# A PEER expert product with its two token halves in one 512-column product, and gate stores in sixteen pieces

## The chip, the core and the metric

The kernel runs on one core of a Trainium2 chip. The metric is the device time of one launch in microseconds; the value for the kernel before is 1862.34 us, the median of three runs (1862.03 to 1863.49). Engine names: TensorE (PE in the rows, PEld for its weight loads), VectorE (DVE), ScalarE (ACT), GpSimd (POOL), SyncE (SP, which only issues DMAs). ScalarE and GpSimd issue DMAs too.

## The reference

One layer over 256 latent tokens (and 256 context tokens) of width 2048: adaLN modulation, a token mixer with RG-LRU scans and a spatial gating unit, an output projection, then a PEER expert layer and a final RMSNorm. The change lies in the expert layer:

```
q   = h @ w_q                                  # per token: 8 heads x 2 halves x 128
s1, s2 = q half 0 · k1, q half 1 · k2          # 128 scores each, per head
v1, i1 = top16(s1);  v2, i2 = top16(s2)
sc, flat = top16(v1[i] + v2[j])                # 16 of 256 pairs, per head
idx = e1 * 128 + e2;  g = softmax(sc)          # 128 (expert, gate) pairs per token, of 16384 experts
act = gelu(h · u_tab[idx])
out = sum over pairs of g * act * v_tab[idx]
```

## The kernel before, in words

**Number format.** Products have fp32 accuracy by splitting each operand into a high part and a low part (`split`, L245 to L261: ScalarE copies the high part, L252, VectorE subtracts to get the low part, L253). `mm3` (L280 to L283) makes three TensorE products from it: high weights with high tokens, high weights with low tokens, low weights with high tokens. Weights arrive as 1 MB tiles in four raw slots, loaded by SP (`emit_load`, L92), each when the split of the tile four places earlier is done. Split halves rotate through five slots of 1024 columns; a tile is split two steps before it is used.

**The expert stage.** The first expert product is dense: all 16384 experts for all 256 tokens, in 128 steps of 128 experts (`u_step`, L1164). A step is 16 blocks of `mm3`, 48 products of 256 columns, into one of four banks; then ScalarE takes the Gelu from the bank (L1176) and stores it (L1177) as 256 columns of the DRAM table `agd`, whose row holds for one expert the activations and the gates of the 256 tokens.

**The fill.** Each step ends with `fill`, which issues some 3000 ns worth of side work, by estimates written into the generators (`beneath`, L1147): the routing (top-16 and softmax, VectorE nearly alone), `list_tables`, the dense gate matrix (`gates`, L1035), the place of each used expert in a compact list (`places`), and the list itself (`make_list`). The work per step does not depend on how long a step takes. `gates` goes in blocks of 8 tokens: two one-hot matrices (L1021) and one scaled (L1030) on VectorE, 24 products of 128 columns (L1041, L1044), and two ScalarE copies into one of two chunk buffers `GC` (L1051). After 8 blocks (64 tokens, one chunk; four chunks in all) ScalarE issues four stores of 1 MB each, in runs of 256 bytes (L1056).

**The second expert product.** The list has 92 tiles of 128 experts. For each, GpSimd fetches the rows of the value table (`gather`, L910) and of `agd` (`act_rows`, L913) by indirect DMA; gate times activation (L1187) gives the weights, split by L1196 and L1201, and `mm3` with 512 columns adds into the output banks. Table fetches 0 to 3 are issued from the fill, the following ones by `emit_load` when the slot that they fill is free. Between the stages stands a branch on the list's overflow (`tc.If`, L1255), not taken with this input: two row fetches are issued ahead of it, the next ones behind it.

**Order.** The program is written out by hand; each engine, and each engine's DMA queue, works through its own instructions in program order and waits on semaphores.

Of the kernel before, what the change touches and what calls it, by code (L numbers as in the profile page):

```python
# [14 lines left out]
ALU = mybir.AluOpType  # L15
# [35 lines left out]
def layer_kernel(ctx: ExitStack, tc: tile.TileContext, I, out, dbg=None):  # L51
# [15 lines left out]
    def q_(off, n):  # L67
        assert O_Q + off + n <= N_F
        return fa[:, O_Q + off:O_Q + off + n]

    def r_(off, n):
        assert O_RP + off + n <= N_R
        return ra[:, O_RP + off:O_RP + off + n]
# [3 lines left out]
    def small(n):  # L77
        o = sm_used[0]
        sm_used[0] += n
        assert sm_used[0] <= N_SM  # L80
        return fa[:, o:o + n]
# [6 lines left out]
    order = []  # L88
    pos = [0]
    loaded = set()  # L90

    def emit_load(i):  # L92
        if i < len(order):
            loaded.add(i)
            key, parts = order[i]
            if parts is None:
                if key[1] + N_RAW < N_L:
                    gather(key[1] + N_RAW)
                return
            base = O_RAW + (i % N_RAW) * D  # L100
            for o, n, src in parts:
                nc.sync.dma_start(fa[:, base + o:base + o + n], src)
# [173 lines left out]
    def behind():  # L276
        if pending:
            pending.pop()()
# [507 lines left out]
    G.dma_start(KY[:, 1024:2048], I["k2t"])  # L786


    HH = r_(0, 4096).rearrange("p (k t) -> p k t", k=KD)
    HL = r_(4096, 4096).rearrange("p (k t) -> p k t", k=KD)  # L790
    HF = [q_(256 * i, 256) for i in range(4)]
    def norm2(k):
        b = pb[4 + k % 4]
# [88 lines left out]
    LIST, LIST2 = (small(N_L).bitcast(U32) for _ in range(2))  # L882
    AGR = [q_(12288 + 512 * i, 512) for i in range(4)]
    WP = [dg2, eg[:, 0:256]]
    pidx = small(1)
    flag = small(3)

# [22 lines left out]
    def gather(n):  # L910
        by_index(v_raw(n), v_rows, LISTV[:, SEQ[n]:SEQ[n] + 1], NE - 1)
# [120 lines left out]

    def gates():  # L1035
        def products(b):
            counts = pb[4 + b // NB][:, 0:P]
            oj, og = pair(b, P)
            for i in range(TB):
                oa = OHA[b % 2][:, i, :]  # L1040
                TE.matmul(counts, oa, oj[:, i, :], start=b % NB == 0 and i == 0,  # L1041
                          stop=b % NB == NB - 1 and i == TB - 1, skip_group_check=True)
                for q in range(2):
                    TE.matmul(pb[6 + i // 4][:, (i % 4) * P:(i % 4 + 1) * P], oa, og[:, i, q, :],  # L1044
                              start=i % 4 == 0 and q == 0, stop=q == 1, skip_group_check=True)

        def keep(b):
            c, o = divmod(b, HT // TB)
            for x in range(2):
                tl = slice(o * TB + 4 * x, o * TB + 4 * x + 4)  # L1050
                S.activation(GC[c % 2][:, :, tl], pb[6 + x].rearrange("p (t j) -> p j t", j=P), AF.Copy,  # L1051
                             scale=1.0 / GSC)
            if o == HT // TB - 1:
                for x in range(4):
                    cs = slice(32 * x, 32 * x + 32)
                    S.dma_start(ag4[cs, :, c // 2, 1, (c % 2) * HT:(c % 2 + 1) * HT].rearrange("c e i -> e c i"),  # L1056
                                GC[c % 2][:, cs, :])

        for b in range(2 * NB + 2):
            sl = slice(b * TB, (b + 1) * TB)  # L1060
            if b < 2 * NB:
                one_hot(OHA[b % 2], E2T[:, sl], P)
                one_hot(pair(b, P)[0], E1T[:, sl], P)
            yield 2300
            if b < 2 * NB:
                scaled(b, GT[:, sl, :], P)
            if b > 1:
                keep(b - 2)
            if 0 < b <= 2 * NB:
                products(b - 1)  # L1070
            yield 2400
# [50 lines left out]
    def make_list():  # L1122
        bank = pb[6][:, 0:2 * N_L]
        for b in range(NB + 1):
            if b < NB:
                sl = slice(b * TB, (b + 1) * TB)
                one_hot(OHA[b % 2], PM[:, sl], P)
                one_hot(pair(b, N_L)[0], PJ[:, sl], N_L)
                scaled(b, VAL[:, sl, :], N_L)
            if b:  # L1130
                for i in range(TB):
                    TE.matmul(bank, OHA[(b - 1) % 2][:, i, :], OHG[(b - 1) % 2][:, 2 * N_L * i:2 * N_L * (i + 1)],
                              start=b == 1 and i == 0, stop=b == NB and i == TB - 1)
            yield 3700
        V.tensor_copy(PT[0][:, 0:N_L], bank[:, N_L:2 * N_L])
        V.scalar_tensor_tensor(PT[1][:, 0:N_L], bank[:, 0:N_L], float(P), PT[0][:, 0:N_L],
                               op0=ALU.mult, op1=ALU.add)
        V.tensor_copy(LIST, PT[1][:, 0:N_L])
        V.tensor_scalar(PT[0][:, 0:N_L], PT[1][:, 0:N_L], -1.0, 0.0, op0=ALU.add, op1=ALU.max)
        V.tensor_copy(LISTV, PT[0][:, 0:N_L])  # L1140
        V.tensor_scalar(PT[0][:, 0:N_A], PT[1][:, 0:N_A], 2.0, None, op0=ALU.mult)
        V.tensor_scalar(PT[0][:, N_A:N_L], PT[1][:, N_A:N_L], 2.0, 1.0, op0=ALU.mult, op1=ALU.add)
        V.tensor_copy(LIST2, PT[0][:, 0:N_L])
        yield 600


    def beneath():  # L1147
        yield from routing()
        yield from list_tables()
        yield from gates()  # L1150
        yield from places()
        yield from make_list()
        for n in range(N_RAW):
            yield from (0 for _ in starts(NU - 16 + 3 * n))
            gather(n)
            yield 100
# [3 lines left out]
    def starts(n):  # L1160
        while at[0] < n:
            yield

    def u_step(n, fill):  # L1164
        parts = uq.pop(n)
        bank = pb[n % 4][:, 0:T]
        ahead2()
        for k in range(KD):
            h, l = parts[k // 8]
            es = slice((k % 8) * P, (k % 8 + 1) * P)  # L1170
            mm3(bank, h[:, es], l[:, es], HH[:, k, :], HL[:, k, :], k == 0, k == KD - 1)
            if k == 7:
                behind()
        fill()
        st = STAGE[n % 3]
        S.activation(st, bank, AF.Gelu_apprx_tanh)  # L1176
        S.dma_start(ag4[n, :, :, 0, :], st.rearrange("p (t i) -> p t i", t=2))  # L1177


    def users(n):  # L1180
# [52 lines left out]
    for n in range(NU):  # L1233
        at[0] = n
        u_step(n, fill)
        if n in (1, 2):
            scores(n - 1, 1, pb[2 + 2 * n:4 + 2 * n])
        if n == 6:
            V.tensor_tensor(modl[:, 48:64], modl[:, 48:64], bm[:, 80:96], op=ALU.add)
        if n == 8:  # L1240
            m5d = row_to_dram(modl[:, 48:64], "m5d", pb[5])
    at[0] = NU
    for _ in work:
        pass

    for n in range(2):
        act_rows(n)


    V.tensor_reduce(flag[:, 0:1], flag, axis=AX.X, op=ALU.add)  # L1250
# [104 lines left out]

    for n in range(2, 4):
        act_rows(n)
    for n in range(2):
        weights(n)
        weights_high(n)  # L1360
        weights_low(n)
# [91 lines left out]
```

## Time and profile before

| | |
|---|---|
| median of 3 runs | 1862.34 us |
| the profiled execution | 1861.65 us, span 1859.7 us |
| granted clock, mean over the span | 0.971 |
| TensorE, VectorE, ScalarE, GpSimd busy | 93%, 70%, 47%, 14% |
| expert products (L281 to L283) on the chain | 23% each |
| DMA, mean over the span | 254 GB/s |

The page gives busy times per engine and the chain of work that ended last. A window row gives the busy time of each engine in one stretch, with the granted clock as a share of full speed and the mean share of the DMA engines. A timeline row gives start, duration, engine (q: its queue, which issues DMAs), line and shape, and in brackets how long the engine had been idle and what ended that. The second expert product begins at 1468 us, the first one at 588 us.

### The profile page before, as it was taken

The numbers are of one execution on the slowest core, as the hardware profiler recorded it, in microseconds if no ns is written. First come the engines' busy times: TensorE is split into PE (matmuls) and PEld (weight loads), VectorE is DVE, ScalarE is ACT, GpSimd is POOL, SyncE is SP. The second block draws the span as 40 slices with busy tenths as digits, with TensorE's granted clock in tenths as the row PEclk, the third lists the DMA queues.
The fourth block names the chain that finished last, engine by engine and source line by source line (L and its number), as shares of the span: only waits on it lengthen the run. The fifth ranks groups of instructions, "written<-read, shape, count | busy, mean of one in ns | idle before, by whom it ended". The sixth has DMA issues, their size and how long they took to land.

```text
span 1859.7 us, 30150 instructions
## 1 busy us (share of the span) xinstructions
PE 1723.9 (93%) x12361; PEld 1539.2 (83%) x12361; DVE 1304.4 (70%) x1804; ACT 868.8 (47%) x1104; POOL 252.3 (14%) x221
## 2 busy tenths in 40 slices
PE   4999999999999999997969979699999799999995
PEld 0778567888899999997969979699999688888884
DVE  1347696887879999885848574588644477777776
ACT  5224666643544444443434343334344456656654
POOL 0000000000100000000000000000100366656662
PEclk9999999999999999998989989799999899999998
DMA  9886868888796766557575766655766589888882
GB/s 389 321 320 255 323 272 320 325 318 332 288 338 239 240 225 203 191 184 210 178 213 170 202 195 187 184 192 190 253 235 204 195 317 340 311 306 306 308 307 80
DMA packets 165512, 472.67 MB, mean 254 GB/s; under 512 B 75924, under 2 KB 108872, under 8 KB 115192
## 3 DMA queue, kind: packets, MB, share of 16 engines
q1 hardware_dynamic: 42624, 303.58, 45.4%
q0 software_dynamic: 21120, 128.68, 19.5%
q10 hardware_dynamic: 101624, 38.42, 8.0%
q8 instruction: 98, 1.61, 0.3%
q14 instruction: 46, 0.38, 0.1%
HBM read 432.81 MB, written 37.83 MB: 253 GB/s over the span
## 4 chain that ended last, share of the span: by engine, by line
PE 76%; DVE 8%; DMA 6%; ACTq 5%; ACT 3%; issue 2%; POOL 0%; SPq 0%; DVEq 0%; POOLq 0%
PE bank L281 23%; PE bank L283 23%; PE bank L282 23%; ACTq L1056 4%; DVE ra L253 2%; DMA fa<-in_wm_a_dram 2%; PE bank L1044 2%; ACT ra L252 1%; DMA fa<-in_wm_c_dram 1%; PE bank L361 1%; PE bank L306 1%; DVE fa L287 1%; PE bank L524 1%; ACTq L1177 1%; PE bank L1041 1%
## 5 line engine op out<-in xcount | busy, mean ns | idle before, releaser
L281 PE MATMUL bank<-ra 128*128 128x256 f32 (+1 forms) x3412 | 1059.5, 311 | 15.4 <-ACT ra L1196 14.3
L283 PE MATMUL bank<-ra 128*128 128x256 f32 (+1 forms) x3412 | 1048.6, 307 | 7.3 <-DVE ra L1201 4.6
L282 PE MATMUL bank<-ra 128*128 128x256 f32 (+1 forms) x3412 | 1047.4, 307 | 1.3 <-DVE ra L253 1.3
L253 DVE TENSOR_TENSOR ra<-fa,ra 128x1024 fp32r<-128x1024 f32 x564 | 683.1, 1222 | 398.9 <-ACT ra L252 393.5
L252 ACT ACTIVATE ra<-fa 128x1024 fp32r<-128x1024 f32 x564 | 592.4, 1058 | 520.2 <-PE bank L282 214.2
L281 PEld LDWEIGHTS bank<-ra 128*128 128x128 f32 x3412 | 656.1, 192 | 73.8 <-issue 25.5
L283 PEld LDWEIGHTS bank<-ra 128*128 128x128 f32 x3412 | 655.0, 192 | 40.0 <-DVE ra L1201 7.4
L282 PEld LDWEIGHTS bank<-ra 128*128 128x128 f32 x3412 | 656.0, 192 | 31.1 <-DVE ra L253 2.4
L1176 ACT ACTIVATE fa<-bank 128x256 f32<-128x256 f32 x128 | 49.1, 383 | 258.6 <-PE bank L283 191.9
L894 POOL DMA_INDIRECT fa<-in_peer_v_dram,fa x92 | 97.0, 1054 | 352.2 <-DVE ra L253 175.7
L894 POOL DMA_INDIRECT fa<-agd,fa x92 | 130.2, 1416 | 37.0 <-issue 26.5
L1021 DVE TENSOR_TENSOR fa<-fa 128x1024 f16<-128x1024 bf16 x96 | 108.1, 1168 | 0.0
L1030 DVE TENSOR_TENSOR fa<-fa 128x2048 f16<-128x2048 f16 (+1 forms) x48 | 100.2, 2088 | 0.8
L1044 PE MATMUL bank<-fa 128*128 128x128 f16 x512 | 49.8, 227 | 40.2 <-ACT fa L1051 24.9
L1044 PEld LDWEIGHTS <-fa 128*128 128x128 f16 x512 | 41.6, 102 | 40.6 <-issue 40.6
L1111 POOL DMA_DIRECT2D ptab<-fa x1 | 0.6, 581 | 546.5 <-DVE fa L1107 546.5
L287 DVE SCALAR_TENSOR_TENSOR fa<-fa 128x2048 f32<-128x2048 f32 x32 | 72.8, 2282 | 0.0
L361 PE MATMUL bank<-fa 128*2 128x512 f32 x256 | 40.7, 729 | 25.1 <-DMA fa<-in_wm_a_dram 16.8
L1196 ACT ACTIVATE ra<-fa 128x128 fp32r<-128x128 f32 x92 | 32.4, 352 | 48.7 <-DVE fa L1187 48.5
L1187 DVE TENSOR_TENSOR fa<-fa 128x128 f32<-128x128 f32 x92 | 33.6, 365 | 24.5 <-DMA fa<-agd,fa 24.1
L1041 PE MATMUL bank<-fa 128*128 128x128 f16 x256 | 47.9, 228 | 0.0
L306 PE MATMUL bank<-fa 128*2 128x512 f32 x256 | 34.1, 620 | 8.8 <-DMA fa<-in_wm_c_dram 8.8
(256 smaller groups left out, 960.2 us busy)
## 6 DMA issues: line engine op xcount, KB each, us to landing
fa<-in_peer_u_dram SPq DMA_DIRECT2D x128, 1024.0 KB, 5.1
fa<-in_wm_a_dram SPq DMA_DIRECT2D x32, 1024.0 KB, 7.7
fa<-in_wm_c_dram SPq DMA_DIRECT2D x32, 1024.0 KB, 7.1
fa<-in_wm_d_dram SPq DMA_DIRECT2D x32, 1024.0 KB, 6.5
fa<-in_w_in_dram SPq DMA_DIRECT2D x24, 1024.0 KB, 5.1
fa<-in_w_out_dram SPq DMA_DIRECT2D x16, 1024.0 KB, 7.1
fa<-in_wq_dram SPq DMA_DIRECT2D x16, 1024.0 KB, 7.1
agd<-fa ACTq DMA_DIRECT2D x128, 128.0 KB, 4.4
```

Source lines behind the costliest of these rows:

```text
L252: S.activation(h, x, AF.Copy)
L253: V.tensor_tensor(l, x, h.bitcast(F32), op=ALU.subtract)
L281: TE.matmul(dst, wh, mh, start=first, stop=False, skip_group_check=skip)
L282: TE.matmul(dst, wh, ml, start=False, stop=False, skip_group_check=skip)
L283: TE.matmul(dst, wl, mh, start=False, stop=last, skip_group_check=skip)
L287: V.scalar_tensor_tensor(junk, w, 1.0, s, op0=ALU.mult, op1=ALU.mult, accum_out=dst)
L894: G.indirect_dma_start(out=dst, out_offset=None, in_=src, in_offset=bass.IndirectOffsetOnAxis(ap=idx, axis=0), bounds_check=bound, oob_is_ ...
L1021: V.tensor_tensor(dst, iota_b[:, 0:n].unsqueeze(1).to_broadcast([P, TB, n]), numbers.unsqueeze(2).to_broadcast([P, TB, n]), op=ALU.is_equal)
L1030: V.tensor_tensor(og, oj.unsqueeze(2).to_broadcast([P, TB, 2, n]), factors.unsqueeze(3).to_broadcast([P, TB, 2, n]), op=ALU.mult)
L1041: TE.matmul(counts, oa, oj[:, i, :], start=b % NB == 0 and i == 0, stop=b % NB == NB - 1 and i == TB - 1, skip_group_check=True)
L1044: TE.matmul(pb[6 + i // 4][:, (i % 4) * P:(i % 4 + 1) * P], oa, og[:, i, q, :], start=i % 4 == 0 and q == 0, stop=q == 1, skip_group_check ...
L1056: S.dma_start(ag4[cs, :, c // 2, 1, (c % 2) * HT:(c % 2 + 1) * HT].rearrange("c e i -> e c i"), GC[c % 2][:, cs, :])
```

## The change

In `u_step` the two products that share the high weights become one: the high and low tokens lie side by side in one array (`H2`), and a 512-column product puts both results into the two halves of a bank. The product of the low weights with the high tokens adds into the first half. The halves are then added: in the first eight steps by a ScalarE copy of the second half and a VectorE sum, later by a ScalarE copy of the whole bank and a GpSimd sum. The Gelu and its store move behind the next step's products (`u_out`). Each chunk of the gates is stored in sixteen pieces of 256 KB, one per step by SP and one in every third step by ScalarE. Table fetches 6 and 7 move from the end of the first expert product to behind the row fetches, one ahead of the branch and one behind it.

```diff
             if parts is None:
-                if key[1] + N_RAW < N_L:
+                if key[1] in (2, 3):
+                    late.append(key[1] + N_RAW)
+                elif key[1] + N_RAW < N_L:
                     gather(key[1] + N_RAW)
...
-    HH = r_(0, 4096).rearrange("p (k t) -> p k t", k=KD)
-    HL = r_(4096, 4096).rearrange("p (k t) -> p k t", k=KD)
+    H2 = r_(0, 8192).rearrange("p (k z t) -> p k z t", k=KD, z=2)
+    HH, HL = H2[:, :, 0, :], H2[:, :, 1, :]
...
+    HALVES = q_(13824, 512)
...
+    def store_piece(eng):
+        if pieces:
+            c, x = pieces.pop(0)
+            cs = slice(8 * x, 8 * x + 8)
+            eng.dma_start(ag4[cs, :, c // 2, 1, (c % 2) * HT:(c % 2 + 1) * HT].rearrange("c e i -> e c i"),
+                          GC[c % 2][:, cs, :])
...
         def keep(b):
             c, o = divmod(b, HT // TB)
+            if o == 0:
+                while pieces and pieces[0][0] < c - 1:
+                    store_piece(S)
...
             if o == HT // TB - 1:
-                for x in range(4):
-                    cs = slice(32 * x, 32 * x + 32)
-                    S.dma_start(ag4[cs, :, c // 2, 1, (c % 2) * HT:(c % 2 + 1) * HT].rearrange("c e i -> e c i"),
-                                GC[c % 2][:, cs, :])
+                pieces.extend((c, x) for x in range(16))
...
         yield from make_list()
+        while pieces:
+            yield 0
...
     def u_step(n, fill):
         parts = uq.pop(n)
-        bank = pb[n % 4][:, 0:T]
+        bank = pb[n % 4]
         ahead2()
         for k in range(KD):
             h, l = parts[k // 8]
             es = slice((k % 8) * P, (k % 8 + 1) * P)
-            mm3(bank, h[:, es], l[:, es], HH[:, k, :], HL[:, k, :], k == 0, k == KD - 1)
+            TE.matmul(bank, h[:, es], H2[:, k, :, :].rearrange("p z t -> p (z t)"), start=k == 0, stop=False,
+                      skip_group_check=True)
+            TE.matmul(bank[:, 0:T], l[:, es], HH[:, k, :], start=False, stop=k == KD - 1, skip_group_check=True)
             if k == 7:
                 behind()
+        store_piece(nc.sync)
+        if n % 3 == 0:
+            store_piece(S)
         fill()
+        u_out(n - 1)
         st = STAGE[n % 3]
-        S.activation(st, bank, AF.Gelu_apprx_tanh)
-        S.dma_start(ag4[n, :, :, 0, :], st.rearrange("p (t i) -> p t i", t=2))
+        if n < 8:
+            S.activation(st, bank[:, T:2 * T], AF.Copy)
+            V.tensor_tensor(st, bank[:, 0:T], st, op=ALU.add)
+        else:
+            S.activation(HALVES, bank, AF.Copy)
+            G.tensor_tensor(st, HALVES[:, 0:T], HALVES[:, T:2 * T], op=ALU.add)
+
+    def u_out(n):
+        if n >= 0:
+            st = STAGE[n % 3]
+            S.activation(st, st, AF.Gelu_apprx_tanh)
+            S.dma_start(ag4[n, :, :, 0, :], st.rearrange("p (t i) -> p t i", t=2))
...
+    u_out(NU - 1)
...
     for n in range(2):
         act_rows(n)
+    gather(late.pop(0))
...
     for n in range(2, 4):
         act_rows(n)
+    gather(late.pop(0))
```

## Rows read from the trace of the kernel before

**Rows 1.** The page: the chain that ended last, share of the span by engine.
```profile
PE 76%; DVE 8%; DMA 6%; ACTq 5%; ACT 3%; issue 2%; POOL 0%; SPq 0%; DVEq 0%; POOLq 0%
```

**Rows 2.** Windows of 40 us: length, engines' busy us (xcount), PEclk, DMA share, GB/s.
```profile
850.00:890.00 40.00, 27.50 (x250) 27.25 (x249) 18.88 (x16) 11.40 (x17) 0.00 (x0) 0.83 0.82 212
950.00:990.00 40.00, 24.70 (x211) 24.49 (x210) 17.76 (x14) 10.28 (x14) 0.00 (x0) 0.79 0.80 208
1050.00:1090.00 40.00, 27.57 (x256) 27.32 (x255) 20.44 (x16) 12.46 (x18) 0.00 (x0) 0.83 0.83 212
1150.00:1190.00 40.00, 19.73 (x150) 19.53 (x149) 12.72 (x30) 8.24 (x11) 0.00 (x0) 0.74 0.75 190
1000.00:1040.00 40.00, 40.00 (x385) 39.83 (x385) 32.38 (x25) 17.93 (x24) 0.00 (x0) 1.00 0.55 178
```

**Rows 3.** Timeline of ScalarE around 860 us: start, duration, engine, line, operation, [idle before].
```profile
853.79 16.74 ACTq L1056 DMA_DIRECT2D agd<-fb  x4
870.58 0.38 ACT L1176 ACTIVATE fa<-bank 128x256 f32<-128x256 f32 x1 [16.82 <-issue]
```

**Rows 4.** Windows in order: routing, routing, gates, list. Columns PE, PEld, DVE, ACT, POOL.
```profile
588.00:641.00 53.00, 51.25 (x420) 50.15 (x419) 53.00 (x176) 23.35 (x29) 0.00 (x0) 1.00 0.69 236
641.00:757.00 116.00, 116.00 (x969) 115.84 (x968) 107.78 (x250) 55.22 (x67) 0.66 (x2) 1.00 0.66 214
795.70:849.60 53.90, 53.90 (x514) 53.69 (x512) 42.73 (x33) 25.73 (x35) 0.00 (x0) 1.00 0.55 182
1211.00:1332.00 121.00, 121.00 (x1050) 120.36 (x1048) 100.89 (x91) 47.88 (x58) 0.00 (x0) 1.00 0.58 187
```

**Rows 5.** Timeline of TensorE in the last step of the first expert product.
```profile
1454.84 0.28 PE L282 MATMUL bank<-ra 128*128 128x256 f32 x1
...
1457.36 0.28 PE L282 MATMUL bank<-ra 128*128 128x256 f32 x1
```

**Rows 6.** Timeline of TensorE in the second expert product.
```profile
1599.98 0.39 PE L281 MATMUL bank<-ra 128*128 128x512 f32 x1
...
1603.83 0.39 PE L283 MATMUL bank<-ra 128*128 128x512 f32 x1
```

**Rows 7.** Groups of ScalarE by shape: xcount | busy us, mean ns | idle before.
```profile
L1051 ACT ACTIVATE fb<-bank 128x512 f32<-128x512 f32 x32 | 17.0, 584 | 0.0
```

**Rows 8.** Timeline near the end, where GpSimd and VectorE sum side by side.
```profile
1817.10 0.69 DVE L1332 TENSOR_TENSOR fb<-fb 128x512 f32<-128x512 f32 x1 [0.22 <-DMA fb<-x1d]
...
1817.71 0.68 DVE L1331 TENSOR_TENSOR fb<-bank,fa 128x512 f32<-128x512 f32 x1
...
1817.88 1.29 POOL L1335 TENSOR_TENSOR fb<-fb,fa 128x512 f32<-128x512 f32 x1 [7.17 <-DVE fb L1332]
...
1818.43 1.29 DVE L1332 TENSOR_TENSOR fb<-fb 128x512 f32<-128x512 f32 x1
```

**Rows 9.** Groups of VectorE by line, 588 to 757 us: the costliest.
```profile
L253 DVE TENSOR_TENSOR ra<-fa,ra 128x1024 fp32r<-128x1024 f32 x60 | 70.7, 1213 | 6.9 <-ACT ra L252 6.9
```

**Rows 10.** Timeline from the last Gelu into the second expert product.
```profile
1457.38 0.99 POOL L894 DMA_INDIRECT fa<-in_peer_v_dram,fa  x1 [4.77 <-DVE fa L1252]
...
1457.79 0.38 ACT L1176 ACTIVATE fa<-bank 128x256 f32<-128x256 f32 x1 [1.94 <-PE bank L283]
...
1465.96 1.00 POOL L894 DMA_INDIRECT fa<-agd,fa  x1 [0.30 <-issue]
...
1468.22 0.80 PE L281 MATMUL bank<-ra 128*128 128x512 f32 x1 [10.46 <-ACT ra L1196]
...
1470.56 1.00 POOL L894 DMA_INDIRECT fa<-agd,fa  x1 [3.60 <-DMA fa<-in_peer_v_dram,fa]
...
1476.41 0.50 PE L283 MATMUL bank<-ra 128*128 128x512 f32 x1 [0.67 <-DVE ra L1201]
```

**Rows 11.** Line L894, issues of 1428 to 1458 us: the table fetches' landing.
```profile
DMA to landing us min/median/max: 5.7/5.9/6.1
```

**Rows 12.** Line L894, issues of 1464 to 1467 us: the row fetches' landing.
```profile
DMA to landing us min/median/max: 2.8/2.8/2.9
```

More of the change, by code (lines that the diff above doesn't have):

```diff
@@ L90, in layer_kernel @@
     loaded = set()
+    late = []
     def emit_load(i):
@@ L1031, in scaled @@
                         factors.unsqueeze(3).to_broadcast([P, TB, 2, n]), op=ALU.mult)
+    pieces = []
+    def store_piece(eng):
[4 more added lines that the diff above has]
+                          GC[c % 2][:, cs, :])
     def gates():
@@ L1244, in layer_kernel @@
         pass
+    assert not pieces
     for n in range(2):
         act_rows(n)
+    gather(late.pop(0))
     V.tensor_reduce(flag[:, 0:1], flag, axis=AX.X, op=ALU.add)
```

## The prediction

> **What bounds the kernel now.** I read the page first: TensorE holds 76% of the chain that ended last [rows 1], so time goes down only where TensorE gets shorter or stands still less. The windows over the expert stage (588 to 1458 us) show where it stands still. A quiet stretch of 40 us has 40 us of TensorE busy and 385 products; four stretches of the same length, about 100 us apart, have 27.5, 24.7, 27.6 and 19.7 us and 867 products together instead of 1540, with the granted clock at 0.74 to 0.83 [rows 2]. The ScalarE timeline names the cause: four gate stores in a row hold ScalarE's queue from 853.79 to 870.5, 4.2 us each, and the Gelu behind them idles 16.8 us "until issue" [rows 3]. Splits of the next weights are queued there too, so VectorE and TensorE run dry. The last thing to see is VectorE: in 588 to 641 it is busy 53.0 of 53 us, in 641 to 757 107.8 of 116 with TensorE at 116 [rows 4]: in the routing both are full. Later it is busy 42.7 of 53.9 us (gates) and 100.9 of 121 (list).
>
> **The change part by part.** The sum is made against the profiled execution, 1861.65 us (span 1859.7), which is 0.7 us under the median 1862.34.
>
> *Gate stores in sixteen pieces: -67 us.* The four stretches miss 1540 - 867 = 673 products; at 40/385 = 0.104 us that is 70 us: 60.5 us of standing still and the rest at the lower clock [rows 2]. The 64 pieces have a quarter of a store, so I price each at 4.2/4 = 1.05 us of its queue. About 48 go to SP, one a step; behind each waits only the load of a weight tile several steps ahead (four raw slots). About 16 go to ScalarE, one every third step, 0.35 us a step; behind them wait the fill's copies, the delayed Gelu and then the next split. ScalarE has room: 25.7 us busy in eight steps, 3.2 a step [rows 4], plus 0.35, a bank copy of 0.58 and its store makes under 5 of 6.5 us. (The 514 products of that window are eight steps of 48 and 130 of the gates, so a step there takes 6.7 us.) A chunk's pieces drain in 12 steps, the next chunk takes about 12.5, and its buffer is asked for one or two steps later still, so nobody should wait for a landing. I leave 2 to 3 us: the fourth stall ends in products that wait for VectorE's counts, and that round trip stays. Bounds: -70 (all) to -58 (one more wait of 3 us at each chunk).
>
> *One 512-column product for two of 256: -20 us.* In the pure steps 21 intervals from 1454.84 to 1457.36 take 2.52 us, 0.120 each [rows 5]; 17 intervals of 512 columns from 1599.98 to 1603.83 take 3.85 us, 0.2265 each [rows 6]. A pair at 0.240 becomes 0.2265, 13.5 ns saved; 16 a step make 0.216 us (5.76 to 5.54). The remaining 256-column product keeps its 0.120, and its weights load beside a longer product than now. The Trainium skill has another price (TensorE: Matmul & The Clock Gate, Back-to-back issue gap): columns over 2.4 plus about 2.5 ns, by which the merge saves 2.5 ns and not 13.5, 0.04 us a step. The rows differ from it at both lengths, 0.120 for its 0.109 and 0.2265 for its 0.216, and the rows decide; the case without the gain is a rival below. The 100 steps after the routing would give 21.6 us; I take off 1.6 because the first gate steps start with no lead of VectorE over TensorE. In the gates VectorE works 42.7/8 = 5.3 us a step, in the list 100.9/19 = 5.3 (1050 products are 19 steps and 138 others) [rows 4], and with 0.65 us more, below, it stays under TensorE's new 6.5 and 6.15. Bounds: 0 to -27 (all 128 steps).
>
> *Adding the halves: +3 us, in the routing.* A ScalarE copy of 512 columns from a bank takes 0.58 us [rows 7]; ScalarE has the room above. The first eight steps add on VectorE, with one operand from a bank: 0.68 us for 512 columns [rows 8], so about 0.40 for 256, 8 x 0.40 = 3.2 us on the engine that is full there. From step 8 GpSimd adds: 1.29 us for 512 columns [rows 8], 0.65 for 256. Its cost on VectorE is in the same rows: a sum of two SBUF operands takes 0.69 us alone and 1.29 when it starts 0.55 us into GpSimd's. It ends 0.55 us after GpSimd does, so it waited; the product with one operand from a bank, at 1817.71 and also beside GpSimd, did not. So each add can hold VectorE for up to 0.65 us. In the routing the weight splits alone are 70.7 of 160.8 us of VectorE's time [rows 4, 9], with the other two-input work about 0.6; over the 20 steps from 641 to 757 (5.76 us each) that is 20 x 0.65 x 0.6 = 8 us. Spare is 116 - 107.8 = 8.2 us [rows 4]. 3.2 + 8 - 8.2 = +3. So the routing, some 28 steps, does not get its 6 us from the merge and becomes 3 us longer: VectorE is late next there. Bounds: -6 (no add blocked, TensorE's saving passed on) to +8 (every add blocked, 13 us).
>
> *End of the stage: +7 us.* Now the last bank's Gelu starts at 1457.79 and the first value product at 1468.22 [rows 10]; between them lie the store, its landing and the first row fetch. After the change copy (0.58), add (0.65) and hand-overs come ahead of that Gelu: +1.35. Table fetches 6 and 7 move from steps 124 and 125 to behind the row fetches; the sixth is issued ahead of the branch. At present GpSimd issues its second row fetch at 1465.96, and the third, the first one behind the branch, only at 1470.56, 3.60 us idle; the table fetch that the row names was issued at 1457.38 and lands within 6.1 us, so GpSimd waited there for its latest fetch, which lands 2.8 us after issue [rows 10 to 12]. With a table fetch as the latest, issued 1.3 us later and landing after 5.9, the third row fetch is 1.3 + 5.9 - 2.8 = 4.4 us later. Its weights feed tile 2, where TensorE already idles 0.67 us at 1476.41 [rows 10]. TensorE would stand still there some 5 us and start on the lower clock (+1). Sum 1.35 + 4.4 + 1 = 6.8. Taking fetches 6 and 7 out of the last steps gives nothing back: TensorE runs through those steps. Bounds: 0 (no such wait, add hidden) to +12 (fetch 7, now ahead of row fetch 4, stops TensorE once more).
>
> *Costed at nothing:* the interleaved layout of the activations (same widths; cover is VectorE's, as before), the wait for the last piece (all drained some 35 steps before the end), table fetches 0 to 3, which now queue behind GpSimd's adds and so come at steps 112 to 121, still ahead of their use; late, each would cost its 5.9 us.
>
> Sum: 1861.65 - 67 - 20 + 3 + 7 = 1784.65, with 0.7 for the median **1785 us**.
>
> **The rivals.**
> 1. *The merge gains nothing*: weight loads or the change of length set a floor, and 512 + 256 columns take the 0.360 us that three products took. For it: products of unlike length do not alternate in any row. Against: 13 ns sit on each product at both lengths [rows 5, 6]. Time 1785 + 20 = 1805. By the skill's 2.5 ns it would be 1785 + 20 - 4 = 1801.
> 2. *VectorE bounds the gates and the list too*: every add costs its 0.65 us there because VectorE's work comes in lumps (two-input work nearly throughout). For: the routing is full. Against: 1.2 us a step are free [rows 4]. Half of the adds of some 78 steps, 25 us, and part of the merge: about 1815.
> 3. *The pieces still hold a queue*: ScalarE's sixteen stop the splits, or a buffer's landing is awaited twice. 16 x 1.05 = 17 us: 1802.
> 4. *Slower*: the add does not get its turn while VectorE has two-input work, and the copy of the next bank, which needs the scratch half, stands in ScalarE's queue ahead of the next split. Then a step becomes the chain VectorE 5.3 + add 0.65 + copy 0.58 + ScalarE's half of a split, taken as long as VectorE's 1.2 [rows 9], = 7.7 us where I have 6.5, over some 78 steps with fill: 1785 + 94 = 1879. It decides from 77/78 = 1 us a step on. For: rows show VectorE waiting for GpSimd, none the reverse. Against: splits leave VectorE idle in each step. The skill (SBUF — State Buffer, Who interferes with whom) has the lock exclusive in both orders, first come first; by that the add waits for one instruction at most, and no run here shows it yet.
>
> **How the numbers follow.** Forecast 0.66, rival 1 0.09, rival 2 0.11, rival 3 0.10, rival 4 0.04. The forecast's own range is 1774 to 1798. The bounds added up reach from 1759 to 1823; leaving out both tails I give 1769 to 1808, which holds rivals 1 and 3. What a measurement here can tell from no change is about 0.2%, 3.7 us. All but rival 4 is faster by far more: faster 0.95, within 0.2% 0.01, slower 0.04.
>
> **What would show it.** Right: no window of 40 us in 850 to 1190 with TensorE under 37 us; pure steps at 5.54 us with spacings 0.2265 and 0.120; VectorE full up to about 760 us with the routing no shorter; an idle time of 4 to 6 us of TensorE about two value tiles after the branch. Wrong: a step of 5.76 us (rival 1); VectorE over 95% in the gates (2, 4); ScalarE or SP issues of over 2 us (3); TensorE without a gap at the third value tile (my end term). Under 1765 the routing and the end would both have cost nothing.

## The result, and the profile after

The changed kernel takes **1791.57 us** (median of 4, 1789.62 to 1794.17); the kernel before, run beside it, 1862.18 us. The ratio is 0.9623, with a 95% interval from 0.9604 to 0.9642. The forecast was 1785 us in a range from 1769 to 1808.

The profiled execution is the one of 1794.17 us (span 1792.4 against 1859.7). The page's chain by engine, which answers to [rows 1], no longer has ScalarE's queue (it was 5%):

```profile
PE 80%; DVE 11%; DMA 5%; issue 2%; ACT 2%; POOL 0%; SPq 0%; DVEq 0%; POOLq 0%; ACTq 0%
```

The four windows of [rows 2] in the changed kernel (length, busy us of PE, PEld, DVE, ACT, POOL, then the granted clock, DMA share, GB/s):

```profile
850.00:890.00 40.00, 40.00 (x293) 34.96 (x292) 35.55 (x26) 21.79 (x34) 9.65 (x6) 1.00 0.71 210
950.00:990.00 40.00, 40.00 (x292) 35.07 (x290) 35.51 (x26) 20.82 (x31) 9.72 (x6) 1.00 0.83 235
1050.00:1090.00 40.00, 40.00 (x292) 34.97 (x291) 35.10 (x24) 21.79 (x33) 10.70 (x7) 1.00 0.88 243
1150.00:1190.00 40.00, 40.00 (x249) 34.63 (x249) 36.97 (x30) 18.85 (x26) 8.01 (x7) 1.00 0.81 243
```

TensorE stands still in none of them, and its clock stays at 1.00 where it had sunk to 0.74 to 0.83.

To see what each part is worth I cut both traces at the first product of a step (step 0 to 127 of the first expert product) and at the first value product:

| stretch | before us | after us | difference | put down to |
|---|---|---|---|---|
| up to step 0 | 588.1 | 587.5 | -0.6 | not touched |
| steps 0 to 28 (routing) | 174.6 | 180.0 | +5.4 | merge -3.1, more waits +8.3 |
| steps 29 to 81 (gates) | 417.2 | 345.6 | -71.6 | stalls -66, merge -5.7 |
| steps 82 to 105 (list) | 150.9 | 146.2 | -4.7 | rest of the last stall -2, merge -2.6 |
| steps 106 to 126 | 121.0 | 118.7 | -2.2 | merge |
| step 127, to the first value product | 16.4 | 16.5 | +0.1 | |
| the rest | 391.5 | 397.8 | +6.4 | the moved table fetches |

So the stalls gave 68 us, the merge about 10 from step 29 on, and routing and end took 12 of that back. Each length is read from one trace. The kernels below that have the changed kernel's code ahead of step 0 take between 582.2 and 591.1 us up to there, and the routing, with the same code too, takes 180.0 us here and 178.5 in `merge_only`; a difference of that size in one trace shows nothing.

The merge first. In a pure step (one without products of other work) the products start like this (start, duration; compare [rows 5] and [rows 6]):

```profile
1380.91 0.40 PE L1188 MATMUL bank<-ra 128*128 128x512 f32 x1
1381.15 0.28 PE L1190 MATMUL bank<-ra 128*128 128x256 f32 x1
1381.26 0.40 PE L1188 MATMUL bank<-ra 128*128 128x512 f32 x1
1381.49 0.28 PE L1190 MATMUL bank<-ra 128*128 128x256 f32 x1
1381.61 0.40 PE L1188 MATMUL bank<-ra 128*128 128x512 f32 x1
1381.85 0.28 PE L1190 MATMUL bank<-ra 128*128 128x256 f32 x1
1381.97 0.40 PE L1188 MATMUL bank<-ra 128*128 128x512 f32 x1
```

Three pairs take 1.06 us, 353 ns a pair; the sum of the two spacings of before, 226.5 and 120, is 346.5. The time varies with a period of three pairs: 361, 350, 350. A step is 5.653 us long, not 5.544.

The routing next. Its two windows, which answer to the first two of [rows 4], and what the products waited for in them:

```profile
588.00:641.00 53.00, 49.35 (x286) 42.41 (x287) 53.00 (x179) 21.64 (x31) 0.00 (x0) 1.00 0.64 231
641.00:757.00 116.00, 112.41 (x623) 96.07 (x622) 110.90 (x251) 64.03 (x89) 22.75 (x20) 0.99 0.59 200
...
its engine sat idle before it (us, times) until:
  DVE ra L256: 5.0, 9
  DVE fa L996: 2.3, 1
```

VectorE is full, and TensorE waits for it: for the low halves of the weights (L256) and for the gates that are transposed (L996). Line 1204 is GpSimd's add, in three stretches by turns: the routing from 640 on, the gates, and the quiet steps (mean ns of one behind the comma):

```profile
L1204 POOL TENSOR_TENSOR fa<-fa 128x256 f32<-128x256 f32 x19 | 22.9, 1205 | 251.6 <-ACT fa L1203 251.6
...
L1204 POOL TENSOR_TENSOR fa<-fa 128x256 f32<-128x256 f32 x46 | 67.7, 1471 | 227.5 <-ACT fa L1203 227.5
...
L1204 POOL TENSOR_TENSOR fa<-fa 128x256 f32<-128x256 f32 x25 | 19.1, 764 | 98.3 <-ACT fa L1203 98.1
```

Beside VectorE's two-input work an add takes on average up to twice the 0.73 us that it takes alone. One place shows who waits for whom:

```profile
679.83 2.29 DVE L987 TENSOR_TENSOR fa<-fa 128x2048 bf16<-128x2048 f32 x1
...
680.03 2.68 POOL L1204 TENSOR_TENSOR fa<-fa 128x256 f32<-128x256 f32 x1 [1.73 <-ACT fa L1203]
682.03 1.76 DVE L256 TENSOR_TENSOR ra<-fa,ra 128x1024 fp32r<-128x1024 f32 x1
```

The add starts 0.2 us into a product of VectorE and needs 2.68 us instead of 0.73: it ends at 682.7, 0.6 us behind the end of that product, so it had stood still until then. The other long adds look the same: 78 of GpSimd's 120 take over 0.8 us, and each of them ends 0.55 to 0.75 us behind the end of a VectorE instruction. VectorE's next split then takes 1.76 us instead of 1.21 [rows 9], for the add is done only at 682.7. Each waits for the other's instruction, whichever came first, as the Trainium skill has it (SBUF — State Buffer, Who interferes with whom); the trace agrees in both orders.

The end of the stage, which answers to [rows 10]:

```profile
1383.58 1.00 POOL L898 DMA_INDIRECT fa<-in_peer_v_dram,fa  x1 [3.87 <-DVE fa L1288]
...
1383.93 0.60 ACT L1203 ACTIVATE fa<-bank 128x512 f32<-128x512 f32 x1 [1.57 <-PE bank L1190]
1384.62 0.73 POOL L1204 TENSOR_TENSOR fa<-fa 128x256 f32<-128x256 f32 x1
1385.38 0.42 ACT L1209 ACTIVATE fa<-fa 128x256 f32<-128x256 f32 x1 [0.85 <-POOL fa L1204]
...
1392.34 1.01 POOL L898 DMA_INDIRECT fa<-agd,fa  x1 [0.30 <-issue]
1393.65 1.00 POOL L898 DMA_INDIRECT fa<-in_peer_v_dram,fa  x1 [0.30 <-issue]
...
1400.94 1.00 POOL L898 DMA_INDIRECT fa<-agd,fa  x1 [6.29 <-DMA fa<-agd,fa]
...
1404.53 0.50 PE L284 MATMUL bank<-ra 128*128 128x512 f32 x1 [2.15 <-ACT ra L1229]
```

The third row fetch comes 8.60 us behind the second (4.60 before), with GpSimd idle for 6.29 us. The row names the row fetches, but the last of these had landed at 1395.74; table fetch 6 landed at 1399.28, 1.7 us ahead of the third row fetch. In [rows 10, 12] the second row fetch, then the latest, landed as long ahead of the third (1.8 us).

### The profile page after: what moved, and what is told of

Read it like the earlier page. It is cut to its first block, busy times and chain, and to the rows that moved or that the text cites. A ratio compares the mean times of both kernels' runs of the same rounds, so it can differ in the third digit from the quotient of the medians.

```text
span 1792.4 us, 26487 instructions
## 1 busy us (share of the span) xinstructions
PE 1707.9 (95%) x10313; PEld 1422.4 (79%) x10313; DVE 1340.4 (75%) x1812; ACT 922.0 (51%) x1232; POOL 401.5 (22%) x341
## 4 chain that ended last, share of the span: by engine, by line
PE 80%; DVE 11%; DMA 5%; issue 2%; ACT 2%; POOL 0%; SPq 0%; DVEq 0%; POOLq 0%; ACTq 0%
PE bank L1188 23%; PE bank L284 13%; PE bank L286 12%; PE bank L285 12%; PE bank L1190 12%; DVE ra L256 4%; DMA fa<-in_wm_a_dram 2%; DMA fa<-in_wm_c_dram 2%; PE bank L1057 2%; PE bank L364 1%; PE bank L309 1%; DVE fa L290 1%; DVE fa L942 1%; PE bank L527 1%; DVE fa L940 1%
## 5 line engine op out<-in xcount | busy, mean ns | idle before, releaser
L256 DVE TENSOR_TENSOR ra<-fa,ra 128x1024 fp32r<-128x1024 f32 x564 | 702.0, 1259 | 291.9 <-ACT ra L255 286.2
L1188 PE MATMUL bank<-ra 128*128 128x512 f32 x2048 | 731.9, 401 | 0.0
L1190 PE MATMUL bank<-ra 128*128 128x256 f32 x2048 | 576.9, 282 | 5.1 <-DVE ra L256 5.0
L284 PE MATMUL bank<-ra 128*128 128x512 f32 (+1 forms) x1364 | 475.0, 348 | 17.9 <-ACT ra L1229 16.8
L286 PE MATMUL bank<-ra 128*128 128x512 f32 (+1 forms) x1364 | 468.2, 343 | 5.4 <-DVE ra L1234 4.5
L285 PE MATMUL bank<-ra 128*128 128x512 f32 (+1 forms) x1364 | 467.8, 343 | 1.4 <-DVE ra L256 1.4
L1188 PEld LDWEIGHTS bank<-ra 128*128 128x128 f32 x2048 | 385.8, 188 | 92.6 <-ACT ra L255 0.2
L1190 PEld LDWEIGHTS bank<-ra 128*128 128x128 f32 x2048 | 387.7, 189 | 8.5 <-DVE ra L256 8.4
L284 PEld LDWEIGHTS bank<-ra 128*128 128x128 f32 x1364 | 261.8, 192 | 76.7 <-issue 25.8
L1204 POOL TENSOR_TENSOR fa<-fa 128x256 f32<-128x256 f32 x120 | 150.9, 1258 | 724.2 <-ACT fa L1203 724.1
L286 PEld LDWEIGHTS bank<-ra 128*128 128x128 f32 x1364 | 261.5, 192 | 36.7 <-DVE ra L1234 6.5
L285 PEld LDWEIGHTS bank<-ra 128*128 128x128 f32 x1364 | 261.8, 192 | 32.1 <-DVE ra L256 3.1
L1203 ACT ACTIVATE fa<-bank 128x512 f32<-128x512 f32 x120 | 71.8, 598 | 145.8 <-PE bank L1190 139.8
L1034 DVE TENSOR_TENSOR fa<-fa 128x2048 f16<-128x2048 f16 (+1 forms) x48 | 109.2, 2275 | 0.8
L1209 ACT ACTIVATE fa<-fa 128x256 f32<-128x256 f32 x128 | 52.0, 407 | 33.7 <-DVE fa L1201 25.6
L364 PE MATMUL bank<-fa 128*2 128x512 f32 x256 | 39.6, 711 | 25.5 <-DMA fa<-in_wm_a_dram 17.4
```

The lines of the kernel that those rows point to most:

```text
L256: V.tensor_tensor(l, x, h.bitcast(F32), op=ALU.subtract)
L284: TE.matmul(dst, wh, mh, start=first, stop=False, skip_group_check=skip)
L285: TE.matmul(dst, wh, ml, start=False, stop=False, skip_group_check=skip)
L286: TE.matmul(dst, wl, mh, start=False, stop=last, skip_group_check=skip)
L1034: V.tensor_tensor(og, oj.unsqueeze(2).to_broadcast([P, TB, 2, n]), factors.unsqueeze(3).to_broadcast([P, TB, 2, n]), op=ALU.mult)
L1188: TE.matmul(bank, h[:, es], H2[:, k, :, :].rearrange("p z t -> p (z t)"), start=k == 0, stop=False, skip_group_check=True)
```

## The experiments

Theory: the pieces are worth the four stalls; the merge is held back by a slower pace of unequal products; the adds make VectorE late in the routing; the moved fetches cost the end. The rivals stand with each run. The stage lengths below are cut as in the table above.

**The pieces alone, and all but the pieces.** `pieces_only` is the kernel before with

```diff
-                for x in range(4):
-                    cs = slice(32 * x, 32 * x + 32)
-                    S.dma_start(...)
+                pieces.extend((c, x) for x in range(16))
```

and `store_piece` in the steps; `merge_only` is the changed kernel with the four lines back.

> The kernel before with its gate copies stored in sixteen pieces each, by the steps, and nothing else changed. Theory: the four stalls go and the rest stands: 66 to 70 us off, 1792 to 1796 us, which is the changed kernel's time within 3 us, so that merge, adding of the halves and the moved fetches together are worth nothing. Rival (the parts of the change that came beside the pieces are a gain of 10 us or more): over 1800 us.

Measured: 1793.78 us, ratio 0.9637 (0.9620 to 0.9653). The gates take 350.7 us instead of 417.2; routing and end are as before within 1.7 us.

> The four stores of a gate copy are large again, all else as changed. Theory (the pieces gave the 66 to 68 us of the four stalls and touch nothing else): the stalls are back, four 40-us windows have TensorE under 37 us, and the time is 1856 to 1864 us, within 6 us of the kernel before. Rival (the pieces gave less and the merge more): under 1850 us.

Measured: 1860.22 us against 1861.39, ratio 1.000 (0.9985 to 1.0016). The stalls are back (windows, columns as above):

```profile
845.00:885.00 40.00, 25.14 (x169) 22.01 (x167) 19.03 (x14) 11.37 (x17) 4.93 (x4) 0.79 0.82 215
940.00:980.00 40.00, 24.11 (x177) 21.16 (x177) 17.71 (x14) 12.33 (x19) 5.24 (x4) 0.79 0.81 202
```

So the pieces are the whole gain. Merge, adding and moved fetches together change nothing that can be measured: what the one gives, the others take. Which property of the pieces does it, their size, their coming one at a time or their moving to SP's queue, these two runs don't separate (more on this under *Stalls* below).

**Does the alternation of lengths cost the merge?** `grouped` has eight 512-column products and then eight 256-column ones in each half of a step:

```diff
+        for x in range(2):
+            for k in range(8):
+                TE.matmul(bank, h[...], H2[:, 8 * x + k, ...], ...)
+            for k in range(8):
+                TE.matmul(bank[:, 0:T], l[...], HH[:, 8 * x + k, :], ...)
```

> The merge gave 0.107 us a step instead of 0.216: a 512-column product and a 256-column one take 353 ns together where 346.5 were booked. Here each half of a step has its eight 512-column products first and then its eight 256-column ones, so that the lengths change 4 times a step instead of 32. Theory A (each change of length costs): the spacings come back to 226.5 and 120 ns, a pure step takes 5.55 to 5.57 us instead of 5.65, the kernel is 9 to 12 us faster than the changed one (about 1781). Rival B (the wide product itself is dearer here, from its bank, its operand or its own weights): spacings of 236 and 117 ns stay whatever the order, step 5.65, time within 2 us of the changed kernel's 1791.6.

Measured: 1786.10 us, ratio 0.9592 (0.9572 to 0.9611); a pure step 5.587 us, 349 ns a pair. That is between the two paces, 353 and 346.5: 0.066 us a step are won of the 0.109 that were missing. Of the eight wide products the last three have 226 to 227 ns, the first five 229 to 236, so the wide product is not dearer by itself (rival B falls). But theory A falls too as it was put. Four changes of length a step cost 0.043 us over 5.544, 11 ns each; thirty-two would then cost 0.34 us, and they cost 0.109. And two other traces have stretches at 346.6 ns with all thirty-two changes: steps 17 to 27 of `undo_late` (below) and steps 57 to 80 of `merge_only`. Here is the first, against quiet steps of the same kernel, 55 us of pure steps each (the first number in brackets counts the products):

```profile
701.00:756.00 55.00, 55.00 (x319) 48.12 (x318) 53.05 (x127) 31.43 (x43) 10.86 (x10) 1.00 0.58 195
1270.00:1325.00 55.00, 55.00 (x313) 47.65 (x312) 23.31 (x19) 28.82 (x40) 10.51 (x12) 1.00 0.72 254
```

The changed kernel has 313 and 314 in the same windows. The first window is the busier one for VectorE, and the changed kernel goes slowly through it with the same load (VectorE 52.62 us, DMA share 0.58), so the load of other engines does not make the slower pace. The products are the same, in the same order; what is left as a difference is how the stretch was entered. In these traces the quicker pace begins and ends at a stop of TensorE, or where products of other work come between. So the strict alternation has two paces, 346.6 and 353.4 ns a pair, and keeps the one it fell into up to such a place.

**Another order.** `palin` turns every second pair round:

```diff
+            if k % 2:
+                TE.matmul(bank[:, 0:T], l[:, es], HH[:, k, :], ...)
             TE.matmul(bank, h[:, es], H2[:, k, :, :]..., ...)
-            TE.matmul(bank[:, 0:T], l[:, es], HH[:, k, :], ...)
+            if k % 2 == 0:
+                TE.matmul(bank[:, 0:T], l[:, es], HH[:, k, :], ...)
```

> The changed kernel with the two products of every second pair in the other order (512, 256, 256, 512, ...), so that the lengths change half as often. In the traces so far the same pair ran at two paces: 353 ns in the changed kernel, and 347 ns in stretches behind a stall (11 steps of the kernel with early table fetches, 25 of the one with large stores); the kernel with the products in groups of eight has 349. Theory P (the strict alternation can lock into a slower rhythm, a period of three pairs; another order can't): pairs of 347 to 349 ns, steps of 5.55 to 5.59, 7 to 12 us faster than the changed kernel. Rival C (each change of length costs 3.3 ns, so 16 instead of 32 changes a step): 350 ns, step 5.60, 5 to 6 us faster. Rival D (the wide product costs it): 353 ns, no gain.

Measured: 1782.72 us, ratio 0.9572 (0.9559 to 0.9585), 8.9 us under the changed kernel. Every pure step is at 348 ns a pair, 5.57 us, as P had it; no stretch falls back (windows as above; below them the products, where a new round of four starts every 0.70 us, and x2 is the two wide ones that now meet):

```profile
701.00:756.00 55.00, 55.00 (x317) 48.02 (x316) 51.71 (x110) 31.57 (x42) 10.91 (x11) 1.00 0.63 211
1270.00:1325.00 55.00, 55.00 (x317) 48.02 (x316) 24.43 (x20) 28.40 (x40) 11.49 (x13) 1.00 0.76 268
```

```profile
1299.73 0.63 PE L1190 MATMUL bank<-ra 128*128 128x512 f32 x2
1300.20 0.28 PE L1193 MATMUL bank<-ra 128*128 128x256 f32 x1
1300.32 0.27 PE L1189 MATMUL bank<-ra 128*128 128x256 f32 x1
1300.43 0.62 PE L1190 MATMUL bank<-ra 128*128 128x512 f32 x2
```

**One length only.** `two_512` gives the low weights 512 columns too (they also meet the low half of the tokens, which adds work):

```diff
-            TE.matmul(bank[:, 0:T], l[:, es], HH[:, k, :], ...)
+            TE.matmul(bank, l[:, es], H2[:, k, :, :]..., ...)
```

> The changed kernel with the low weights also over 512 columns (they meet the low half of the tokens too, which adds work), so that all products of a step have one length. Theory P (the slower pace needs a change of length): all spacings are 226 to 227 ns, a pure step 7.25 us, in all steps the same. Rival (the wide product at 512 columns from these operands has a second pace by itself): spacings of 232 to 241 ns in part of the steps, steps of 7.4 us or more.

Measured: 1988.06 us; all spacings 226 or 227 ns, every pure step 7.254 us. With one length there is one pace, here as with three products of 256 before (5.76 us in every pure step). So the slower pace belongs to the alternation. What in TensorE holds it there the runs don't settle; that it is the loading of weights beside a shorter product is only a guess, and was not tried.

**The adds in the routing.** `no_add_routing` leaves the adding out of steps 0 to 28 (`if n < 29: S.activation(st, bank[:, 0:T], AF.Copy)`).

> The changed kernel, whose halves are not added for the first 29 steps (the low part of the tokens is left out of those 29 blocks; the copy takes 256 columns instead of 512, and neither GpSimd nor VectorE adds). Theory (VectorE bounds the routing, and the adds, its own eight and GpSimd's twenty-one in its way, make it 5 to 8 us late, for which TensorE waits 8.3 us more than before): the first 29 steps take 171 to 173 us instead of 180.0, TensorE's waits in them fall from 10 to about 2 us, and the kernel is 7 to 9 us faster than the changed one. Rival (the waits come from ScalarE's longer queue, a copy and a later Gelu, which stay): the 29 steps stay at 178 us or more.

Measured: 1782.34 us, ratio 0.9587 (0.9563 to 0.9612), 9.2 us under the changed kernel; its five executions lie between 1779.7 and 1792.4, so the stage lengths of the profiled one (1781.2 us) have to carry the argument. Some 5 us there are its steps 31 to 81, which fell into the quicker pace (the gates take 340.3 us). The 29 steps take 173.6 us, just over what was expected, and TensorE's waits in them (starts over 0.33 us apart, less 0.23) are 5.0 us; they were 10.2 in the changed kernel and 1.9 before. In 588 to 757 us, where the changed kernel has 161.76 us of TensorE:

```profile
588.00:757.00 169.00, 165.25 (x943) 142.76 (x944) 161.22 (x429) 83.77 (x121) 0.66 (x2) 1.00 0.64 221
...
its engine sat idle before it (us, times) until:
  DVE ra L256: 2.6, 6
  DVE fa L996: 1.3, 1
```

The adds are the larger part of the loss, as the theory said; 3 us of waits more than before stay without them, for TensorE now asks for its weights 0.107 us a step earlier of a VectorE that is still full.

`v_add_29` has VectorE add up to step 28 (`if n < 29:` for `if n < 8:`).

> VectorE adds the halves of the first 29 steps instead of the first 8, and GpSimd those from 29 on. Theory (a GpSimd add keeps VectorE off for longer than VectorE's own add of 0.40 us takes): steps 8 to 28 lose 2 to 4 us less, the first 29 take 176 to 178.5 us instead of 180.0. Rival (the adds on GpSimd lie beside VectorE's one-input work and cost it under 0.4 us each): the 29 steps take 180 us or more, for 21 times 0.40 is 8.4 us more on the engine that bounds them.

Measured: 1789.26 us (1781.3 to 1794.2), ratio 0.9599 (0.9576 to 0.9621); the 29 steps take 177.9 us. That is 2.1 us under the changed kernel but only 0.6 under `merge_only`, which has the same adds, so a gain isn't shown. What it shows is that 21 adds of 0.40 us on the full VectorE (8.4 us) make the routing no longer than 21 adds on GpSimd do: one of these costs VectorE about as much as an add of its own.

`old_to_29` goes back to three narrow products, and to no adding, up to step 28:

```diff
+        if n < 29:
+            for k in range(KD):
+                mm3(bank[:, 0:T], h[:, es], l[:, es], HH[:, k, :], HL[:, k, :], k == 0, k == KD - 1)
+        else:
```

> The first 29 steps by the three 256-column products of the kernel before, with no adding; from step 29 on as changed. Theory (each of these steps is 0.107 us longer, but the 8.3 us of waits go): the 29 steps take 174 to 175.5 us, as in the kernel before, and the kernel is 4 to 6 us faster than the changed one, about 1786. Rival (the delayed Gelu or the pieces make the routing longer, not the adds): 178 us or more, no gain.

Measured: 1786.08 us, ratio 0.9590 (0.9577 to 0.9603); the 29 steps take 174.66 us, before 174.61. Where VectorE has no time left the merge costs more than it gives.

**The moved fetches.** `undo_late` issues table fetches 6 and 7 in the last steps again:

```diff
-                if key[1] in (2, 3):
-                    late.append(key[1] + N_RAW)
-                elif key[1] + N_RAW < N_L:
+                if key[1] + N_RAW < N_L:
...
-    gather(late.pop(0))
```

> Table fetches 6 and 7 are issued early again, as in the kernel before, all else as changed. Theory (GpSimd stands at the branch until fetch 6 has landed, so the third row fetch is issued 4 us later): the wait of 3.1 us at the branch goes, the second and third row fetch are 4.6 us apart instead of 8.6, the stores of the last outputs land 1.3 us later, and the stretch behind the first value product is 4 to 6 us shorter: 2 to 5 us faster than the changed kernel. Rival (the early fetches cost as much where they stood, against the last stores and the row fetches): within 1.5 us of the changed kernel or slower.

Measured: 1787.14 us, ratio 0.9599 (0.9583 to 0.9615), 4.4 us under the changed kernel. The second and the third row fetch are 4.60 us apart again, and TensorE doesn't idle there (20 us from the first value product on, first the changed kernel, then this one):

```profile
1394.30:1414.30 20.00, 16.20 (x47) 12.10 (x48) 9.86 (x16) 8.16 (x12) 9.69 (x10) 0.71 0.67 231
```

```profile
1393.70:1413.70 20.00, 19.81 (x73) 15.78 (x74) 14.10 (x21) 11.74 (x17) 10.54 (x11) 0.84 0.58 209
```

The changed kernel gets 47 products done there, this one 73, the one before 74: 26 products at 0.2265 us are 5.9 us. Behind the first value product 391.5 us are left instead of 397.8, so the whole 6.4 us of the table are the moved fetches: 2.5 us more of TensorE standing still (3.55 us against 1.01 before), and most of the rest the lower clock around it, 0.71 against 0.92 in the same 20 us before (and 0.84 here, where TensorE stands still for nothing). All kept traces agree: the five with early fetches have 390.6 to 393.1 us behind the first value product, the eight with moved ones 395.5 to 399.9.

**Together.** `best_17`: steps 0 to 16 narrow without adding, the rest merged in `palin`'s order, fetches early. `best_29`: the same with 29 narrow steps.

> Three things together: steps 0 to 16 by the three narrow products of the kernel before, without adding; steps 17 to 127 merged, every second pair in the other order; table fetches 6 and 7 early as in the kernel before. Theory (the parts add up): the first 17 steps 105.2 us as in the kernel before, steps 17 to 28 67.0 to 67.5 us (VectorE is some 10 us ahead of TensorE's transposes there, which covers twelve adds), routing 172 to 173 us against 180.0; steps 29 to 127 at 5.57 us and 8 us shorter; the end 5 us shorter: 20 us off the changed kernel, about 1771. Rival (twelve adds make VectorE late again at the second set of transposes, and the fetches and stores of the end eat what is won): 1778 or more.

> As the run with 17 narrow steps, but with 29. Theory: the routing takes 174.6 us as in the kernel before, all else as there: about 2 us above that run, 1773. Rival (the adds of steps 17 to 28 cost waits that narrow steps have not): below that run.

Measured: **1771.35 us** (1770.66 to 1774.37), ratio 0.9526 (0.9509 to 0.9542), and 1776.21 us, ratio 0.9557 (0.9538 to 0.9575). The first takes 105.2 us for 17 steps and 172.4 for 29, as expected, and 390.6 us behind the first value product; the second was to be 2 us slower and is 4.9 (2.0 between the two profiled spans). `best_17` beats both kernels, the changed one by 20 us. Its windows (the narrow steps, twelve merged steps with adds, a former stall, quiet steps):

```profile
588.00:693.00 105.00, 103.24 (x852) 102.05 (x852) 103.64 (x286) 46.74 (x59) 0.50 (x1) 1.00 0.65 228
693.00:760.00 67.00, 67.00 (x388) 58.49 (x387) 62.24 (x152) 35.48 (x48) 11.37 (x12) 1.00 0.63 215
850.00:890.00 40.00, 40.00 (x292) 35.26 (x290) 34.10 (x24) 21.45 (x32) 9.43 (x7) 1.00 0.80 230
1270.00:1325.00 55.00, 55.00 (x317) 47.98 (x317) 24.54 (x20) 28.49 (x39) 11.53 (x13) 1.00 0.76 269
```

The adds cost nothing once VectorE has passed the first set of transposes.

## Why the prediction was right, and where a term was off

The forecast was 6.6 us too low: the merge gave 10 us less and routing took 2 more. (The stages are read from the profiled execution, which lies 2.6 us above the median; stalls, end and the stretch up to step 0 came out 2 us better together.) The bounds of the terms add up to 1824 at most, not 1823, which changes nothing.

*Stalls, -67.* Right: -68, and `pieces_only` alone gives it. No piece held a queue as rival 3 has it: the gates have no step over 7.1 us. The price of a piece, though, was read wrongly. [rows 3] merges four stores into one row, and the prediction took a quarter of it, 4.2 us, for each store and a quarter of that, 1.05 us, for a piece. One by one (start, duration, queue, line; L1177 is the store of the Gelu behind them), and then ScalarE's pieces in the changed kernel (shortest, median and longest, in ns):

```profile
853.79 0.41 ACTq L1056
854.24 6.45 ACTq L1056
860.73 4.34 ACTq L1056
...
865.39 5.14 ACTq L1056
...
870.99 3.73 ACTq L1177
```

```profile
L1045 ACTq DMA_DIRECT2D agd<-fb x8: 361/366/404, 875.0 to 1091.2; - x8
```

The first store of 1 MB holds the queue no longer than a piece of 256 KB does, and the Gelu's store of 128 KB, 0.52 us in a quiet step, holds it for 3.73 us when it comes behind the four. It is so at all four stalls: 0.36 to 0.41 us for the first store, 4.15 to 8.16 for the next three, 3.73 to 4.42 for the Gelu's. So a store held the queue when it came right behind large ones, whatever its own size. The forecast came right all the same because the pieces are not only smaller but also come one at a time, and mostly on SP (0.39 to 0.78 us each there, once 1.72). Whether the four large stores, one in each of four steps, would have done as well is an open rival: no run tried it.

*Merge, -20.* The mis-sized term. From step 29 on it gave 10.5 us, 0.107 a step instead of 0.216. The prices of the two products were right: `two_512` has 226.7 ns, the 256-column ones 120 before, and the quicker pace of the pair is their sum, 346.6. What failed is the step from two prices to a pair: I added spacings that were each measured among their like. Rival 1 named the point (no row had unlike products in turn) and took a whole loss for it; half came. The Trainium skill's 2.5 ns of gap (TensorE: Matmul & The Clock Gate, Back-to-back issue gap), which that section gives for isolated products and not for a stream that loads new weights each time, is met by neither pace: by it the merge would save 0.04 us a step, and the runs show 0.107 and, in `palin`'s order, 0.19.

*Adding, +3 in the routing.* Mechanism right, size 5.4. The copy took 0.60 us for 0.58, the add 0.73 for 0.65, and VectorE was late next. The step that failed is the spare 8.2 us, taken from one window over 641 to 757. In the kernel before it lay thus:

```profile
641.00:690.00 49.00, 49.00 (x410) 48.84 (x409) 47.80 (x107) 23.95 (x30) 0.66 (x2) 1.00 0.66 209
690.00:757.00 67.00, 67.00 (x561) 67.00 (x561) 59.98 (x145) 31.27 (x37) 0.00 (x0) 1.00 0.66 217
```

1.2 us up to the first transposes, 7.0 behind them. The transposes at step 16 are a date that VectorE has to keep, and the later spare doesn't help it: the first 17 steps lost 6.7 us, the next 12 won 1.3. `best_17` uses just that.

*End, +7.* The sum right (+6.4 and +0.2), the parts not all. The third row fetch was 4.0 us later for 4.4, and TensorE's idle time grew by 2.5 us, not 4 to 5, but the lower clock cost more than the 1 us I gave it (about 3.4: the 5.9 us of the missing products less the 2.5). The 1.35 us of copy and add did come (the last store was issued 1.5 us later after the last product), but it landed 4.4 us behind its issue instead of 5.7. In the other runs this is 3.7 to 5.9 us, 4.2 in `undo_late` too, so the moved fetches aren't the cause; what is, no run shows.

*Costed at nothing:* no wait for last pieces and none for the early table fetches is seen. Rivals 2 and 4: VectorE works 35.1 to 37.0 of 40 us in the windows above, TensorE waits for nothing, and an add that finds VectorE at work waits until the instruction in its way is done, 2.68 us with its own work at most.

## What to carry to other kernels

A price taken among products of one length holds for a mix only where the mix was measured; a strict alternation can settle in a slower pace, and another order of the same products (here 3 lines) can bring back what is lost. Spare time of a full engine counts only ahead of the date at which somebody waits for it, so cut the window at that date before subtracting. When a change has parts, price each alone: here one part was the whole gain, and three others cancelled. A row that merges several instructions gives no price of one: look at them singly before dividing.

## What was not expected of the hardware

The same sequence of products ran at 346.6 and at 353.4 ns a pair in one execution, at a granted clock of 1.00 in both, for up to 51 steps on end at the quicker pace (`no_add_routing`) and 80 at the slower (the changed kernel). An add of 256 columns on GpSimd took 0.73 us alone, 1.47 on average beside VectorE's two-input work, 2.68 at most. The first of four 1 MB stores in a row held its queue for 0.4 us, and a 128 KB store behind them for 3.7 to 4.4.
